# A new order of work at seven places of a split-fp32 hybrid decoder block

## The chip, the cores and the metric

The kernel runs on one core of one Trainium2 chip. The metric is the device time of one execution in microseconds (us). Before the change three runs gave 1134.07, 1134.16 and 1134.71; the median is 1134.16. The engines are named as in the profile: PE is TensorE (PEld its weight loads), DVE is VectorE, ACT is ScalarE, POOL is GpSimd, SP is SyncE, which issues most transfers.

## The reference, cut to what matters

```python
h = concatenate([meta, x], axis=1)              # 16 meta tokens + 512 tokens, 1024 wide
h = h + 0.5 * swiglu(rmsnorm(h, ffn1_norm), w1, w3, w2)
hn = rmsnorm(h, mix_norm)
q, k, v, u, g_attn, g_ssm = split(hn @ w_in, SPLITS)
attn = sliding_window_attention(q, k, v, attn_sinks)   # 16 query heads, 4 key heads, window 128
y = gelu(s5_ssm(u, ...))
ssm = (y @ ssm_glu_a) * sigmoid(y @ ssm_glu_b)
merged = sigmoid(g_attn) * attn + sigmoid(g_ssm) * ssm
h = h + merged @ w_out
h = h + 0.5 * swiglu(rmsnorm(h, ffn2_norm), w1, w3, w2)  # second set of weights
return rmsnorm(h, final_norm)[:, N_META:]
```

`swiglu(h, w1, w3, w2)` is `(silu(h @ w1) * (h @ w3)) @ w2`, and the hidden width is 2816 (22 tiles of 128).

## The kernel before, in words

All large matrices are multiplied in three parts. An fp32 operand is split into a high part (a copy rounded by ScalarE, tags `whi`, `hgh`, `gh`, `YH`, `KH`) and a low part (the difference, mostly by VectorE: `wlo`, `hgl`, `gl`, `YL`, `KL`). Each product is then high by high, low by high and high by low, three matmuls in one PSUM tile (`mm3`, lines 218 to 231). Activations lie transposed: 128 rows of the model width per tile, 528 columns (512 tokens and 16 meta tokens, as two halves of 264 with 8 meta columns each); behind the meta tokens' last use there are 512.

The weights stream through the core. `load_raw` (line 149) lets SP fetch one block into one of two raw buffers; `prep_piece` splits 128 of its columns, ScalarE the high part (line 166), then VectorE the low part (line 167), into one of three buffers; the last piece of a block also requests the next block. A unit is the work on one piece: `step` issues its matmuls, splits a later piece, and evacuates PSUM. Pieces of other work, the `mids`, are put between a unit's matmuls at even distances (`accumulate`). Each engine runs its own instructions in exactly the order in which the program issues them, so the place of a call in the program decides who stands behind whom. A PSUM tile that ScalarE and VectorE both read is read by one after the other, in program order; a tile that is taken again waits for its last reader.

The stages, with the lines that the change and the prediction touch:

- Head (about 0 to 44 us). `warm` (line 734) issues matmuls on a tile of ones, two instructions a call, in three places with counts `WARM`. The input `x` arrives in four row blocks `xb`; `x_t` (line 763) transposes two 128-column tiles of two row blocks into one of four PSUM buffers tagged "ax" (a pool that other small products share, in turn); `x_hi` (line 767, ScalarE) and `x_lo` (line 771, VectorE) make the split, gain-scaled activations from it, and `x_cp` (lines 778 and 780) copies the plain transposes to `hT`. `x_meta` (line 745) does this for the meta tokens, with one half of the tile that `warm` writes. `first_mm` (line 851) holds the first two units, w1 and w3 of the first hidden tile: unit 0 on column half 0, then unit 1 on half 0, unit 0 on half 1, and unit 1 on half 1, 96 matmuls counted c = 0 to 95. The dictionary of `first_work` names what is issued ahead of which count: the transposes and splits of half 1, the squares of the rows (`sq`, lines 869 and 871), the evacuation of unit 0 (`keep_p`, line 858, into `held0`), the split of the third piece, the copies `x_cp`, and the meta tokens' sums (`sums`, line 884), whose "ax" tile is the next in turn. In unit 2, `diag_r` (line 318) and `bcast_r` (lines 325 to 328) spread each row's norm factor over the partitions, and `small` (lines 862 to 865) brings in the other gains and the sinks.
- Rest of FFN1, then the projections of the mixer (k, v, u), and the state-space layer. `ssm_f` (lines 1094 to 1101) transposes its result and splits it into `YH` and `YL`.
- Mixer units (about 500 to 718 us): 30 units of 24 matmuls of 512 columns, for q, the gates and the two GLU products, in the order `MIX`. Each has 11 cuts, at which the parts of the attention are issued: scores (`s1`, lines 1249 to 1252), softmax (`s3`, with line 1267), transposes and values. `ksplit` (lines 1197 to 1201) splits one key tile, that is two key heads e = 0 and 1, four ScalarE copies and four low parts; `qsplit` (lines 1226 and 1227) does it for query tiles, high parts on ScalarE, low parts on GpSimd. `ksplit(0)` and two `qsplit` stand ahead of the units, `ksplit(1)` in unit 8. Every unit but the first splits one later piece at cut 8. The last units' `msplit` (lines 1389 and 1390) splits the merged result (`merge`, line 1335) for w_out; `glu`'s evacuation is lines 1380 and 1381.
- w_out, FFN2, and the tail (from about 1100 us). The last product is made by column halves in 16 steps j: `tail_mm` (line 1501), evacuation `tail_evac` (lines 1506 to 1517, which scales by the final gain into `zg`, one of five buffers), and transposes back `tail_t` (line 1525), each two steps behind its `tail_evac` in the first half. `tail_out` scales the rows and writes them.

Of the kernel before, what the change touches and what calls it, by code (L numbers as in the profile page):

```python
# [21 lines left out]
CHUNKS2 = [6, 6, 6, 4]  # L22
WARM = (6, 4, 3)
MIX = (
# [4 lines left out]
)  # L29
NCUT = 11  # L30
KS1 = 8
VS = (1, 0, 2, 10, 13, 13)
# [7 lines left out]
T = 8  # L40
# [12 lines left out]
def fr(ap):  # L53
    return ap.bitcast(F32)
# [3 lines left out]
def hybrid_block_kernel(  # L58
# [752 lines left out]
    m_lo = x_meta()  # L811
    warm(WARM[2])
    x_t(0, 2)
# [93 lines left out]
    def first_work():  # L907

        w = {}

        def at(c, f, *a):
            w.setdefault(c, []).append(lambda: f(*a))
        at(24, sums_meta)
        for g in range(2):
            for j in range(2 * g, 2 * g + 2):
                at(28 + 8 * g, x_t, 1, j)
            for d in range(4 * g, 4 * g + 4):
                at(28 + 8 * g, x_hi, 1, d)
                at(28 + 8 * g, x_lo, 1, d)
        for b in range(4):  # L920
            at(52, sq, b)
        at(72, keep_p, 0)
        at(74, prep_piece)
        for j in range(4):
            at(76, x_cp, 1, j, V if j % 2 else S)
        at(80, sums)
        return w

    pairs = first_downs(CHUNKS1)
    for i, u in enumerate(units):  # L930
        mids = ()
        if i == 0:
            work = first_work()
        elif i == 2:
            mids = (lambda: dgs.append(diag_r(x_p)), lambda: bcast_r(ax_ps, dgs[0]), small)
        elif i > 3:
            mids = (lambda: next(side, None),)
        if i in pairs:
            step2(u, units[i + 1], mids)
        elif i - 1 not in pairs:  # L940
            step(*u, hold=i < 3, mids=mids, prep=i > 0)
        if i == 2:
            flush()
            sx.close()
    for _ in side:
# [144 lines left out]
    def ssm_f(b0, q):  # L1090
# [3 lines left out]
        for t in range(4):  # L1094
            PE.transpose(ps[:, 128 * t:128 * t + 128], y[:, 4 * q + t].rearrange("k g c -> k (g c)"), ident)
        src = ps.rearrange("p (t e k) -> p e k t", t=4, e=2)
        for e in range(2):
            oh = YH[:, b0 + e, :].rearrange("p (k t) -> p k t", t=T)[:, :, 4 * q:4 * q + 4]
            ol = YL[:, b0 + e, :].rearrange("p (k t) -> p k t", t=T)[:, :, 4 * q:4 * q + 4]
            S.activation(out=oh, in_=src[:, e], func=AF.Copy)  # L1100
            V.tensor_tensor(out=ol, in0=src[:, e], in1=fr(oh), op=ALU.subtract)

# [88 lines left out]

    def ksplit(m):
        t = kT[m].rearrange("p h c -> p (h c)")
        for e in range(2):
            r = slice(64 * e, 64 * e + 64)
            o = slice(64 - 64 * e, 128 - 64 * e)
            S.activation(out=KH[r, 2 * m + e, :], in_=t[r], func=AF.Copy)
            S.activation(out=KH[o, 2 * m + e, :], in_=t[r], func=AF.Copy)
            eng = G if m else V
            eng.tensor_tensor(out=KL[r, 2 * m + e, :], in0=t[r], in1=fr(KH[r, 2 * m + e, :]), op=ALU.subtract)  # L1200
# [190 lines left out]

    ksplit(0)
    for m in range(2):
# [6 lines left out]
    for i, u in enumerate(units):  # L1400
# [19 lines left out]
        at_cut(CUT["ev"], flush)  # L1420
        at_cut(CUT["ev2"], flush2)
        if i == KS1:
            at_cut(CUT["ks"], ksplit, 1)
            at_cut(CUT["ks"], vmeta, 1)
        for v, iv in enumerate(VS):
            if i == iv:
                at_cut(CUT["vs"], vsplit, *divmod(v, 3))
        if i:
            at_cut(CUT["prep"], prep_piece)
# [4 lines left out]

        step(*u, mids=[lambda fs=fs: [f() for f in fs] for fs in cuts], prep=False, hold=i < len(units) - 1)


# [118 lines left out]
    for j in range(2 * ND):  # L1556
# [9 lines left out]
        tail_evac(p, h, d)  # L1566
        for t in after.get(j, (j - 2,) if 2 <= j < 8 else ()):
            if t not in (14, 15):
                tail_t(*divmod(t, ND))
# [36 lines left out]
```

## Time and profile before

| | |
|---|---|
| median of three runs | 1134.16 us |
| profiled execution | 1134.81 us |
| its span, first to last instruction | 1133.0 us |
| mean granted PE clock | 0.996 |
| PE, PEld, DVE, ACT, POOL busy | 99%, 89%, 56%, 36%, 32% of the span |
| bytes moved by DMA | 108.43 MB, 96 GB/s |

A row of a timeline or a group reads: start or none, busy time, engine, line, operation, output from inputs, partitions by elements and type, count, and in square brackets how long the engine stood idle ahead of it and what released it. Busy times of matmuls that overlap are longer than the step from one start to the next. "issue" as a releaser means that the profile shows nothing that the engine waited for.

### The profile page before, as it was taken

To read this page: it belongs to the slowest core of one execution; us is meant where nothing else is said; L and a number is where in the kernel's file an instruction comes from. 1 tells how busy PE (TensorE), PEld (TensorE's weight loads), DVE (VectorE), ACT (ScalarE), POOL (GpSimd) and SP (SyncE) were. 2 spreads that over 40 slices of the span, in tenths; PEclk is the share of its full clock that TensorE was granted. 3 is DMA by queue.
4 is the path that set the end of the run, shared out by engine and by line. 5 is a ranking of instruction groups with operands and counts; after the bars stand their busy time and mean duration, and the time that the engine had idled before them with its cause. 6 is when DMAs were issued, how large, how long until landed. Compare 5 with 4: busy or idle time off the path is not lost.

```text
span 1133.0 us, 17255 instructions
## 1 busy us (share of the span) xinstructions
PE 1117.9 (99%) x7012; PEld 1004.0 (89%) x7012; DVE 633.4 (56%) x963; ACT 409.2 (36%) x726; POOL 360.4 (32%) x488
## 2 busy tenths in 40 slices
PE   8999999999999999999999999999999999999997
PEld 7999999999999999978888888888888888888887
DVE  5546663655444363878777786554444444444454
ACT  5322232232222242456656555343322222222233
POOL 1777672542884031535455231130000000000003
PEclk9999999999999999999999999999999999999998
DMA  5523233232423246122222212423232223323222
GB/s 155 147 76 111 75 95 113 75 86 84 113 76 102 76 139 200 49 75 75 75 75 70 76 52 101 149 76 110 93 116 89 86 98 114 112 63 123 75 75 75
DMA packets 105903, 108.43 MB, mean 96 GB/s; under 512 B 7568, under 2 KB 102032, under 8 KB 105696
## 3 DMA queue, kind: packets, MB, share of 16 engines
q1 hardware_dynamic: 103424, 100.74, 28.4%
q0 software_dynamic: 2352, 6.52, 2.2%
q8 instruction: 55, 0.90, 0.3%
q14 instruction: 24, 0.20, 0.1%
q10 hardware_dynamic: 48, 0.07, 0.0%
HBM read 100.80 MB, written 5.34 MB: 94 GB/s over the span
## 4 chain that ended last, share of the span: by engine, by line
PE 91%; DVE 4%; ACT 2%; issue 1%; POOL 1%; POOLq 0%; DVEq 0%; ACTq 0%
PE p L231 63%; PE p L405 11%; PE p L407 9%; PE p L1501 1%; PE pv L1310 1%; PE ps_t L1275 1%; DVE wlo L167 1%; PE ps_s L1249 1%; PE ps_s L1250 1%; PE p L851 1%; PE ps L734 1%; DVE hgl L771 0%; POOL qs L1227 0%; ACT hgh L767 0%; ACT whi L166 0%
## 5 line engine op out<-in xcount | busy, mean ns | idle before, releaser
L231 PE MATMUL p<-hgh,whi 128*128 128x264 f32 (+1 forms) x1408 | 403.8, 333 | 0.1
L231 PE MATMUL p<-hgl,whi 128*128 128x264 f32 (+1 forms) x1408 | 402.8, 332 | 0.2 <-DVE hgl L1390 0.2
L231 PE MATMUL p<-hgh,wlo 128*128 128x264 f32 (+1 forms) x1408 | 401.0, 331 | 0.0
L167 DVE TENSOR_TENSOR wlo<-raw,whi 128x1024 fp32r<-128x1024 f32 (+2 forms) x190 | 250.1, 1316 | 84.3 <-ACT whi L166 81.9
L231 PEld LDWEIGHTS p<-hgh,whi 128*128 128x128 f32 x1408 | 239.0, 188 | 26.5 <-issue 1.1
L231 PEld LDWEIGHTS p<-hgh,wlo 128*128 128x128 f32 x1408 | 238.6, 189 | 23.3
L231 PEld LDWEIGHTS p<-hgl,whi 128*128 128x128 f32 x1408 | 238.8, 189 | 22.7 <-DVE hgl L1390 0.5
L166 ACT ACTIVATE whi<-raw 128x1024 fp32r<-128x1024 f32 (+2 forms) x190 | 185.5, 978 | 127.4 <-PE p L407 72.2
L1517 POOL TENSOR_TENSOR acc<-acc,zq 128x256 f32<-128x256 f32 x12 | 8.8, 735 | 349.8 <-ACT zq L1510 349.7
L377 ACT ACTIVATE t<-t 128x528 f32<-128x528 f32 (+1 forms) x44 | 28.1, 639 | 167.0 <-DVE t L376 167.0
L425 DVE SCALAR_TENSOR_TENSOR hT<-p,hT 128x528 f32<-128x528 f32 (+1 forms) x56 | 39.1, 698 | 87.5 <-PE p L407 52.2
L387 ACT ACTIVATE gh<-t 128x528 fp32r<-128x528 f32 (+1 forms) x44 | 28.1, 639 | 161.9 <-DVE t L386 161.9
L405 PE MATMUL p<-gh,whi 128*128 128x264 f32 x352 | 72.5, 287 | 0.7 <-DVE hT L425 0.5
L405 PE MATMUL p<-gl,whi 128*128 128x264 f32 x352 | 71.4, 284 | 0.0
L405 PE MATMUL p<-gh,wlo 128*128 128x264 f32 x352 | 71.4, 284 | 0.0
L376 DVE TENSOR_TENSOR t<-p,r_bc 128x512 f32<-128x512 f32 (+1 forms) x43 | 30.0, 698 | 69.3 <-PE p L231 69.1
L386 DVE TENSOR_TENSOR t<-p,t 128x512 f32<-128x512 f32 (+1 forms) x43 | 30.0, 698 | 66.7 <-PE p L231 66.3
L405 PEld LDWEIGHTS p<-gh,whi 128*128 128x128 f32 x352 | 54.5, 188 | 1.9 <-issue 0.8
L407 PE MATMUL p<-gh,whi 128*128 128x512 f32 x144 | 56.0, 389 | 0.0
L407 PE MATMUL p<-gl,whi 128*128 128x512 f32 x144 | 56.0, 389 | 0.0
L407 PE MATMUL p<-gh,wlo 128*128 128x512 f32 x144 | 56.0, 389 | 0.0
L378 DVE TENSOR_TENSOR t<-t,r_bc 128x528 f32<-128x528 f32 (+1 forms) x44 | 37.3, 848 | 32.4 <-ACT t L377 32.4
(331 smaller groups left out, 1500.3 us busy)
## 6 DMA issues: line engine op xcount, KB each, us to landing
raw<-in_ffn_w_dram SPq DMA_DIRECT2D x42, 1024.0 KB, 5.4
raw<-in_ffn_w_dram SPq DMA_DIRECT2D x24, 768.0 KB, 4.2
raw<-in_w_in_dram SPq DMA_DIRECT2D x16, 1024.0 KB, 5.6
raw<-in_ffn_w_dram SPq DMA_DIRECT2D x10, 512.0 KB, 3.6
raw<-in_w_out_dram SPq DMA_DIRECT2D x4, 1024.0 KB, 5.1
h_keep<-hT POOLq DMA_DIRECT2D x1, 2112.0 KB, 7.3
xb<-in_x_dram SPq DMA_DIRECT2D x8, 256.0 KB, 5.1
raw<-in_ssm_glu_a_dram SPq DMA_DIRECT2D x4, 512.0 KB, 3.5
```

The costliest lines, as they stand in the source:

```text
L166: S.activation(out=hi, in_=src, func=AF.Copy)
L167: V.tensor_tensor(out=lo, in0=src, in1=fr(hi), op=ALU.subtract)
L231: PE.matmul(out=o, lhsT=w[:, k0 + k, :], rhs=sl(r, k), start=start, stop=stop)
L376: V.tensor_tensor(out=t1, in0=cell[1], in1=rb(), op=ALU.mult)
L377: S.activation(out=t1, in_=t1, func=AF.Silu)
L378: V.tensor_tensor(out=t1, in0=t1, in1=rb(), op=ALU.mult)
L386: V.tensor_tensor(out=t3, in0=cell[3], in1=cell["t1"], op=ALU.mult)
L387: S.activation(out=gh, in_=t3, func=AF.Copy)
L405: PE.matmul(out=p[:, h, :HALF], lhsT=wt[:, k, :], rhs=gs[k][c][:, h, :], start=start, stop=stop)
L407: PE.matmul(out=p, lhsT=wt[:, k, :], rhs=gs[k][c].rearrange("p h c -> p (h c)"), start=start, stop=stop)
L425: V.scalar_tensor_tensor(out=hv(hT, d), in0=cell["p"], scalar=0.5, in1=hv(hT, d), op0=ALU.mult, op1=ALU.add)
L734: PE.matmul(out=ps_0[:, 0, 0:128], lhsT=ones, rhs=ones, start=True, stop=True)
```

## The change

1. `WARM` goes from (6, 4, 3) to (6, 2): two of the four calls ahead of the first transposes go, and the third group, ahead of `x_t(0, 2)`, goes altogether.
2. In `first_work`, the four high parts of each group of half 1 come ahead of their four low parts; they alternated. `x_cp` of half 1 moves from c = 76 to 50, the split of the third piece from 74 to 52, the squares from 52 to 54, `sums` from 80 to 88.
3. In unit 2 `diag_r` stays at its quarter, `bcast_r` moves from a half to three quarters, and `small` moves to the middle of unit 3. The head's pool is closed one unit later.
4. `ssm_f` makes both high parts ahead of both low parts.
5. `ksplit(0)` ahead of the mixer units does only key head e = 0. Head e = 1 follows at cut 10 of mixer unit 3 (counted from 0), its low parts on GpSimd instead of VectorE.
6. The last mixer unit no longer splits a piece at cut 8; that piece is split behind the unit's evacuation.
7. The tail's transposes run three steps behind `tail_evac` instead of two, up to j = 8.

```diff
@@ -20,7 +20,7 @@
 EPS = 1e-6
 CHUNKS1 = [4, 6, 6, 6]
 CHUNKS2 = [6, 6, 6, 4]
-WARM = (6, 4, 3)
+WARM = (6, 2)
 MIX = (
     ("q", 1), ("gs", 0), ("glu", 0), ("q", 2), ("ga", 0),
     ("gs", 1), ("glu", 1), ("q", 3), ("ga", 1),
@@ -28,6 +28,7 @@
     ("gs", 3), ("ga", 3), ("glu", 3),
 )
 NCUT = 11
+KS0 = 3
 KS1 = 8
 VS = (1, 0, 2, 10, 13, 13)
 CUT = {"s3": 5, "s3m": 7, "s3e": 7, "ev2": 6, "s1": (2, 4, 7, 7), "s2o": 7, "s2p": 7, "s2m": 8, "prep": 8, "ev": 0, "ks": 10, "vs": 7}
@@ -809,7 +810,6 @@
     x_lo(0, 0)
     x_lo(0, 1)
     m_lo = x_meta()
-    warm(WARM[2])
     x_t(0, 2)
     x_t(0, 3)
     x_lo(0, 2)
@@ -914,16 +914,16 @@
         for g in range(2):
             for j in range(2 * g, 2 * g + 2):
                 at(28 + 8 * g, x_t, 1, j)
-            for d in range(4 * g, 4 * g + 4):
-                at(28 + 8 * g, x_hi, 1, d)
-                at(28 + 8 * g, x_lo, 1, d)
+            for f in (x_hi, x_lo):
+                for d in range(4 * g, 4 * g + 4):
+                    at(28 + 8 * g, f, 1, d)
+        for j in range(4):
+            at(50, x_cp, 1, j, V if j % 2 else S)
+        at(52, prep_piece)
         for b in range(4):
-            at(52, sq, b)
+            at(54, sq, b)
         at(72, keep_p, 0)
-        at(74, prep_piece)
-        for j in range(4):
-            at(76, x_cp, 1, j, V if j % 2 else S)
-        at(80, sums)
+        at(88, sums)
         return w
 
     pairs = first_downs(CHUNKS1)
@@ -932,7 +932,9 @@
         if i == 0:
             work = first_work()
         elif i == 2:
-            mids = (lambda: dgs.append(diag_r(x_p)), lambda: bcast_r(ax_ps, dgs[0]), small)
+            mids = (lambda: dgs.append(diag_r(x_p)), lambda: None, lambda: bcast_r(ax_ps, dgs[0]))
+        elif i == 3:
+            mids = (small,)
         elif i > 3:
             mids = (lambda: next(side, None),)
         if i in pairs:
@@ -941,6 +943,7 @@
             step(*u, hold=i < 3, mids=mids, prep=i > 0)
         if i == 2:
             flush()
+        if i == 3:
             sx.close()
     for _ in side:
         pass
@@ -1094,11 +1097,11 @@
         for t in range(4):
             PE.transpose(ps[:, 128 * t:128 * t + 128], y[:, 4 * q + t].rearrange("k g c -> k (g c)"), ident)
         src = ps.rearrange("p (t e k) -> p e k t", t=4, e=2)
+        oh, ol = [[t[:, b0 + e, :].rearrange("p (k t) -> p k t", t=T)[:, :, 4 * q:4 * q + 4] for e in range(2)] for t in (YH, YL)]
         for e in range(2):
-            oh = YH[:, b0 + e, :].rearrange("p (k t) -> p k t", t=T)[:, :, 4 * q:4 * q + 4]
-            ol = YL[:, b0 + e, :].rearrange("p (k t) -> p k t", t=T)[:, :, 4 * q:4 * q + 4]
-            S.activation(out=oh, in_=src[:, e], func=AF.Copy)
-            V.tensor_tensor(out=ol, in0=src[:, e], in1=fr(oh), op=ALU.subtract)
+            S.activation(out=oh[e], in_=src[:, e], func=AF.Copy)
+        for e in range(2):
+            V.tensor_tensor(out=ol[e], in0=src[:, e], in1=fr(oh[e]), op=ALU.subtract)
 
     def st2():
         s = stats(sqs, ax_ps)
@@ -1189,14 +1192,14 @@
 
     V.tensor_reduce(out=hm, in_=ident.rearrange("p (l h k) -> p h l k", l=2, h=4), axis=mybir.AxisListType.XY, op=ALU.add)
 
-    def ksplit(m):
+    def ksplit(m, es=(0, 1)):
         t = kT[m].rearrange("p h c -> p (h c)")
-        for e in range(2):
+        for e in es:
             r = slice(64 * e, 64 * e + 64)
             o = slice(64 - 64 * e, 128 - 64 * e)
             S.activation(out=KH[r, 2 * m + e, :], in_=t[r], func=AF.Copy)
             S.activation(out=KH[o, 2 * m + e, :], in_=t[r], func=AF.Copy)
-            eng = G if m else V
+            eng = G if m or e else V
             eng.tensor_tensor(out=KL[r, 2 * m + e, :], in0=t[r], in1=fr(KH[r, 2 * m + e, :]), op=ALU.subtract)
             eng.tensor_tensor(out=KL[o, 2 * m + e, :], in0=t[r], in1=fr(KH[r, 2 * m + e, :]), op=ALU.subtract)
 
@@ -1389,7 +1392,7 @@
         S.activation(out=mg[0][:, m, :], in_=AT[:, m, :], func=AF.Copy)
         V.tensor_tensor(out=mg[1][:, m, :], in0=AT[:, m, :], in1=fr(mg[0][:, m, :]), op=ALU.subtract)
 
-    ksplit(0)
+    ksplit(0, (0,))
     for m in range(2):
         qsplit(m, qT[m])
     units = []
@@ -1419,13 +1422,15 @@
                 at_cut(CUT[c], f, begin[i - 1])
         at_cut(CUT["ev"], flush)
         at_cut(CUT["ev2"], flush2)
+        if i == KS0:
+            at_cut(CUT["ks"], ksplit, 0, (1,))
         if i == KS1:
             at_cut(CUT["ks"], ksplit, 1)
             at_cut(CUT["ks"], vmeta, 1)
         for v, iv in enumerate(VS):
             if i == iv:
                 at_cut(CUT["vs"], vsplit, *divmod(v, 3))
-        if i:
+        if 0 < i < len(units) - 1:
             at_cut(CUT["prep"], prep_piece)
         if i == len(units) - 2:
             mg += new_hg(SEQ)
@@ -1433,6 +1438,7 @@
                 at_cut(m, msplit, m)
 
         step(*u, mids=[lambda fs=fs: [f() for f in fs] for fs in cuts], prep=False, hold=i < len(units) - 1)
+    prep_piece()
 
 
     at.close()
@@ -1564,7 +1570,7 @@
         if j == 2 * ND - 1:
             tail_t(1, d - 1)
         tail_evac(p, h, d)
-        for t in after.get(j, (j - 2,) if 2 <= j < 8 else ()):
+        for t in after.get(j, (j - 3,) if 3 <= j < 9 else ()):
             if t not in (14, 15):
                 tail_t(*divmod(t, ND))
         if j == 9:
```

Lines of the changed kernel lie 1 to 6 higher. The three places below show what stands in an engine's row before and after; the numbers behind names are buffer numbers.

ScalarE in the head, from the last high parts of half 1 (`hgh`) to the weight split ahead of unit 2; `whi_353` and `whi_325` are the third piece, `ps_x_266` and `ps_x_261` the tile of `x_t(1, 0)`. Before:

```order
L767 ACTIVATE hgh_104<-ps_x_297,gT_66 128x256 [waits PE_49]
L767 ACTIVATE hgh_104<-ps_x_297,gT_66 128x256 [waits DVE_49]
L869 ACTIVATE xb1_112,ssq_88<-xb1_112 128x1024 [waits DMAHW5_49,DMAHW3_49,Pool_49]
L869 ACTIVATE xb3_114,ssq_88<-xb3_114 128x1024 [waits DMAHW5_49,DMAHW3_49]
L858 ACTIVATE held0_221<-p_231 128x528 [waits PE_49]
L166 ACTIVATE whi_353<-raw_211 128x1024 [waits DMAHW6_49]
L778 ACTIVATE hT_93<-ps_x_266 128x2x256
L778 ACTIVATE hT_93<-ps_x_292 128x2x256
L858 ACTIVATE held1_222<-p_256 128x528 [waits PE_49]
L166 ACTIVATE whi_392<-raw_215 128x1024 [waits DMAHW7_49,Activation_49]
```

After:

```order
L768 ACTIVATE hgh_104<-ps_x_292,gT_66 128x256 [waits PE_49]
L768 ACTIVATE hgh_104<-ps_x_292,gT_66 128x256
L779 ACTIVATE hT_93<-ps_x_261 128x2x256 [waits DVE_49]
L779 ACTIVATE hT_93<-ps_x_287 128x2x256 [waits DVE_49]
L167 ACTIVATE whi_325<-raw_206 128x1024 [waits DMAHW6_49]
L869 ACTIVATE xb1_112,ssq_88<-xb1_112 128x1024 [waits DMAHW5_49,DMAHW3_49,Pool_49]
L869 ACTIVATE xb3_114,ssq_88<-xb3_114 128x1024 [waits DMAHW5_49,DMAHW3_49]
L858 ACTIVATE held0_216<-p_226 128x528 [waits PE_49]
L858 ACTIVATE held1_217<-p_251 128x528 [waits PE_49]
L167 ACTIVATE whi_387<-raw_210 128x1024 [waits DMAHW7_49,Activation_49]
```

The two copies to `hT` stood behind the squares, `held0` and the third piece; they now stand directly behind the last high part, the third piece behind them, and the squares and `held0` last. The last high part waits for PE alone, no longer for VectorE.

ScalarE at the start of the mixer units, the last `ssm_f` parts (`YH`), the key tile (`KH`) and the first two query tiles (`qs`). Before:

```order
L1100 ACTIVATE YH_4773<-psT_5641 128x64x4 [waits PE_49]
L1100 ACTIVATE YH_4773<-psT_5641 128x64x4 [waits DVE_49]
L1100 ACTIVATE YH_4773<-psT_5650 128x64x4 [waits PE_49]
L1100 ACTIVATE YH_4773<-psT_5650 128x64x4 [waits DVE_49]
L1197 ACTIVATE KH_5679<-kT_5140 64x544 [waits DMAHW7_49,DMAHW2_49]
L1198 ACTIVATE KH_5679<-kT_5140 64x544
L1226 ACTIVATE qs_5712<-tq0_5564 64x512 x2
L1226 ACTIVATE qs_5717<-tq0_5635 64x512 x2
```

The two lines of `KH` stand there twice, once for each key head. After:

```order
L1102 ACTIVATE YH_4768<-psT_5636 128x64x4 [waits PE_49]
L1102 ACTIVATE YH_4768<-psT_5636 128x64x4
L1102 ACTIVATE YH_4768<-psT_5645 128x64x4 [waits PE_49]
L1102 ACTIVATE YH_4768<-psT_5645 128x64x4
L1200 ACTIVATE KH_5674<-kT_5135 64x544 [waits DMAHW7_49,DMAHW2_49]
L1201 ACTIVATE KH_5674<-kT_5135 64x544
L1229 ACTIVATE qs_5703<-tq0_5559 64x512 [waits DVE_49]
L1229 ACTIVATE qs_5703<-tq0_5559 64x512
L1229 ACTIVATE qs_5708<-tq0_5630 64x512 [waits DVE_49]
L1229 ACTIVATE qs_5708<-tq0_5630 64x512
```

The second high part of each pair no longer waits for VectorE, and two of the four copies to `KH` are gone from this place.

VectorE in the last mixer unit: GLU evacuation (`tg`, `ts`), merge (`AT`), the last low part for w_out (`hgl`) and weight splits (`wlo`). Before:

```order
L167 TENSOR_TENSOR wlo_7823<-raw_7660,whi_7822 128x1024 [waits Activation_49]
L1380 SCALAR_TENSOR_TENSOR tg_7813<-tg_7813,p_7815 128x512 [waits PE_49]
L1381 SCALAR_TENSOR_TENSOR ts_7671<-ts_7671,tg_7813 128x512 [waits DVE_49]
L1335 SCALAR_TENSOR_TENSOR AT_5683<-ts_7671,AT_5683 128x512 [waits DVE_49]
L1390 TENSOR_TENSOR hgl_7746<-AT_5683,hgh_7745 128x512 [waits Activation_49]
L167 TENSOR_TENSOR wlo_7898<-raw_7737,whi_7897 128x1024 [waits DMAHW1_49,Activation_49]
```

After:

```order
L1393 TENSOR_TENSOR hgl_7741<-AT_5678,hgh_7740 128x512 [waits Activation_49]
L1383 SCALAR_TENSOR_TENSOR tg_7808<-tg_7808,p_7810 128x512 [waits PE_49,Activation_49]
L1384 SCALAR_TENSOR_TENSOR ts_7666<-ts_7666,tg_7808 128x512 [waits DVE_49]
L1338 SCALAR_TENSOR_TENSOR AT_5678<-ts_7666,AT_5678 128x512 [waits DVE_49]
L1393 TENSOR_TENSOR hgl_7741<-AT_5678,hgh_7740 128x512 [waits Activation_49]
L168 TENSOR_TENSOR wlo_7829<-raw_7655,whi_7828 128x1024 [waits Activation_49]
L168 TENSOR_TENSOR wlo_7893<-raw_7732,whi_7892 128x1024 [waits DMAHW1_49,Activation_49]
```

The first `wlo` moved from ahead of the GLU evacuation to behind the low part `hgl`.

## The prediction

> **What bounds the kernel now.** I read the page first, and on it the chain that ended last, by engine.
>
> ```profile
> PE 91%; DVE 4%; ACT 2%; issue 1%; POOL 1%; POOLq 0%; DVEq 0%; ACTq 0%
> ```
>
> PE carries 91% of the chain, and the change removes only four plain matmuls from it and three more at a place where PE waits. So a gain can only come from stretches in which PE waits, or runs at a lower clock. I therefore went through PE's starts in the timeline for steps longer than its usual .23 us for 512 columns or .12 for 264, and asked at each place what released it. The places that the change touches are the head (0 to 35 us), the first attention scores (504 to 508), the end of the mixer (718) and the tail (1106). Of the clock, the stretches of 3.41 us say most; their columns are length, busy time of PE, PEld, DVE, ACT and POOL, granted clock, DMA share and GB/s.
>
> ```profile
> 0.00:3.59 3.59, 2.59 (x12) 2.59 (x12) 0.00 (x0) 1.49 (x2) 2.70 (x13) 1.00 0.47 143
> 3.59:7.00 3.41, 3.15 (x15) 2.83 (x15) 0.17 (x1) 0.00 (x0) 0.52 (x2) 1.00 0.91 261
> 7.00:10.41 3.41, 2.40 (x24) 2.14 (x23) 2.24 (x7) 2.40 (x6) 0.96 (x3) 1.00 1.15 318
> 10.41:13.82 3.41, 2.87 (x23) 2.45 (x20) 3.05 (x8) 3.15 (x8) 0.77 (x2) 1.00 0.59 217
> 24.07:27.48 3.41, 1.68 (x16) 1.57 (x16) 2.66 (x5) 2.23 (x4) 0.00 (x0) 1.00 0.00 0
> 27.48:30.89 3.41, 3.41 (x18) 3.41 (x17) 0.95 (x4) 1.55 (x2) 2.69 (x4) 0.50 0.90 286
> ```
>
> The clock is 0.50 in exactly one stretch of 3.41 us, right behind the one stretch in which PE was busy for only 1.68 of 3.41. A stretch with 2.40 busy (7.00 to 10.41) was followed by full clock.
>
> **The change part by part.** All sums are made against the profiled execution, 1134.81 us (1.8 of it lie around the span), which is .65 above the median 1134.16 and .1 above the slowest of the three timed runs.
>
> Term 1, the warm-up calls in the head:
>
> ```profile
> 4.39 2.07 PE L734 MATMUL ps<-ones 128*128 128x128 f32 x8 [0.26 <-DVE gT L738]
> 6.25 1.41 PE L763 MATMUL ps_x<-ident,xb 128*128 128x128 f32 x8
> 9.26 0.94 PE L734 MATMUL ps<-ones 128*128 128x128 f32 x6 [1.01 <-DVE hT L750]
> 10.67 1.57 ACT L767 ACTIVATE hgh<-ps_x,gT 128x256 fp32r<-128x256 f32 x4 [0.27 <-PE ps_x L763]
> 1.17 0.42 SPq L717 DMA_DIRECT2D xb<-in_x_dram  x1
> xb<-in_x_dram SPq DMA_DIRECT2D x1, 256.0 KB, 4.2
> ```
>
> A call counts as two instructions. Eight of them fill 4.39 to 6.25, so four are .93; the first transposes can start about .9 earlier, at 5.4, where the second x transfer (issued at 1.17, landing 4.2 later) arrives as well. ScalarE's first high parts, and all that hangs on them, move with them. The third call made PE wait 1.01 for VectorE's copy out of the same tile; without it the next transposes are ready early, and ScalarE's wait of .27 goes. Together at most 1.1; I take 1.0. The low bound is .2 (rival 1).
>
> Term 2, high parts ahead of low parts, and term 3, the copies `x_cp` ahead of the squares:
>
> ```profile
> 21.10 0.52 PE L851 MATMUL p<-hgh,whi 128*128 128x264 f32 x3
> 21.86 0.39 PE L851 MATMUL p<-hgh,whi 128*128 128x264 f32 x1 [0.24 <-ACT hgh L767]
> 23.05 1.13 PE L851 MATMUL p<-hgh,whi 128*128 128x264 f32 x8
> 25.23 0.59 ACT L778 ACTIVATE hT<-ps_x 128x512 f32<-128x512 f32 x1
> 25.92 0.24 PE L884 MATMUL ps_mq<-ones,mq 128*8 128x1 f32 x4 [1.73 <-issue]
> ```
>
> PE's fourth matmul would have followed at 21.10 + 3 x .12 = 21.46; it came at 21.86, since each ScalarE high part waited for the VectorE low part of the same PSUM tile. With four high parts in a row that .4 goes (bounds 0, if another part is late, and .5).
>
> The wait of 1.73 before line 884 is put down to "issue", so I looked for who frees its tile. `sums` takes the fourth "ax" buffer in turn, that of ps_x(1,0), whose last reader is the ScalarE copy of line 778: it ends at 25.23 + .59 = 25.82, and PE goes on at 25.92. The copy stood behind two squares, `held0` and a weight's high part. It now stands ahead of them. PE's eight matmuls from 23.05 at .1225 end their issue at 24.03, so 25.92 - 24.03 = 1.9 goes (bounds 1.7, the wait as labelled, and 2.0). What is late next is `held0`, now behind both squares; unit 2 needs its PSUM buffer only after the rest of unit 1, by my count of these durations about 1 us later. `sums` itself moves from 80 to 88, and the squares it needs are done by then.
>
> Term 4, the half clock that follows:
>
> ```profile
> 29.96 0.64 PE L231 MATMUL p<-hgh,whi 128*128 128x264 f32 x2
> 30.41 0.63 PE L231 MATMUL p<-hgl,whi 128*128 128x264 f32 x2
> 31.36 0.40 PE L231 MATMUL p<-hgl,whi 128*128 128x264 f32 x2
> 31.60 0.41 PE L231 MATMUL p<-hgh,wlo 128*128 128x264 f32 x2
> ```
>
> Two matmuls take 30.41 - 29.96 = .45 at half clock and 31.60 - 31.36 = .24 at full clock. The stretch of 3.41 us costs 3.41 x (1 - .24/.45) = 1.6. With the gap of 1.9 gone, the stretch before it is about 3.4 busy instead of 1.68, so I expect the clock to stay, worth 1.5 (bounds 0 and 1.6). The Trainium skill, page "TensorE: Matmul & The Clock Gate", section "HAM oscillation — how this bites in real kernels", has it that only idle gaps longer than about 3.4 us lower the clock; by that rule a gap of 1.9 would not have done it, its removal would not save the 1.5, and the sum would come to 5.85 instead of 7.35. The trace sides with the gap, as the two rows of 1.68 and 0.50 stand next to each other; rival 2 keeps the other case.
>
> The broadcast moves from the middle of unit 2 to its third quarter:
>
> ```profile
> 32.58 0.59 PE L325 MATMUL ps_r<-dg,ones 128*128 128x256 f32 x2
> 34.36 0.51 PE L231 MATMUL p<-hgh,whi 128*128 128x264 f32 x2
> ```
>
> It occupies PE for 34.36 - 32.58 = 1.8 wherever it stands; `small` too only moves. Since unit 2 starts some 4 us earlier while the row factors do not, the broadcast may wait for VectorE's diagonal, 0 to .5; I take 0, as the quarter of a unit of 24 x .24 us gives it 1.4 more. The head gives 1.0 + .4 + 1.9 + 1.5 = 4.8.
>
> Term 5, the attention's start:
>
> ```profile
> 497.60 0.66 ACT L1100 ACTIVATE YH<-psT 128x256 fp32r<-128x256 f32 x2 [1.36 <-DVE YL L1101]
> 499.08 0.65 ACT L1197 ACTIVATE KH<-kT 64x544 fp32r<-64x544 f32 x1
> 502.54 8.07 POOL L1227 TENSOR_TENSOR qs<-tq,qs 64x512 fp32r<-64x512 f32 x6 [12.81 <-ACT qs L1226]
> 503.89 0.33 PE L1249 MATMUL ps_s<-KH,qs 128*128 128x144 f32 x1 [0.58 <-POOL qs L1227]
> 507.95 0.33 PE L1249 MATMUL ps_s<-KH,qs 128*128 128x144 f32 x1 [0.65 <-POOL qs L1227]
> PEld ps_s L1249 <- POOL qs L1227: 2.2, 3, 1.0
> L1200 POOL TENSOR_TENSOR KL<-kT,KH x2: 1360/1536/1711, 567.2 to 570.4; 64x544 fp32r<-64x544 f32 x2
> 529.32 0.63 ACT L1362 ACTIVATE ts<-ts 128x512 f32<-128x512 f32 x1 [2.13 <-DVE ts L1361]
> 534.09 1.90 POOL L1267 TENSOR_TENSOR E<-E,den 128x1024 f32<-128x1024 f32 x1 [4.51 <-ACT ph L1278]
> ```
>
> PE waits .58 and .65 for GpSimd, whose low parts begin at 502.54 after ScalarE. Two of four key copies (.65 each) and waits for VectorE such as the 1.36 leave ScalarE's way to `qs`: it gets there about 3 us earlier, more than PE's waits. So .58 + .65 and a restart of about .1 at each go: 1.4 (bounds 1.2 and the weight loads' 2.2). The second head's parts return in the fourth unit: 2 x .65 on ScalarE, 2 x 1.54 = 3.1 on GpSimd. Queued behind them are the softmax steps; the idle 2.13 and 4.51 in front of 529.32 and 534.09 hide them.
>
> Term 6, the last mixer weight, and term 7, the tail:
>
> ```profile
> 713.57 1.23 DVE L167 TENSOR_TENSOR wlo<-raw,whi 128x1024 fp32r<-128x1024 f32 x1 [0.74 <-ACT whi L166]
> 717.54 0.69 DVE L1390 TENSOR_TENSOR hgl<-AT,hgh 128x512 fp32r<-128x512 f32 x1 [0.70 <-ACT hgh L1389]
> 717.56 0.50 PE L231 MATMUL p<-hgh,whi 128*128 128x512 f32 x1
> 718.29 0.50 PE L231 MATMUL p<-hgl,whi 128*128 128x512 f32 x1 [0.22 <-DVE hgl L1390]
> 1105.34 0.41 DVE L1506 SCALAR_TENSOR_TENSOR z<-p,hT 128x256 f32<-128x256 f32 x1
> 1105.57 0.28 PE L1501 MATMUL p<-gh,hgl 128*128 128x256 f32 x1
> 1106.19 0.44 PE L1525 MATMUL ps_z<-ident,zg 128*128 128x128 f32 x2 [0.35 <-DVE zg L1515]
> ```
>
> The merge and the last low part no longer stand behind a 1.23 us weight part on VectorE. PE's second matmul came .73 after the first instead of .23: .5, with the restart .6 (bounds .5 and .7). The moved weight part ends about when the merge chain ended, before PE's second w_out unit; its raw tile's successor is requested some 3 us later on SP, which has none waiting behind it.
>
> In the tail the transposes at 1106.19 waited for zg, .62 after the matmul of 1105.57 instead of .12. With a lag of three that zg is long there. Next late is the PSUM buffer that VectorE frees at 1105.34 + .41 = 1105.75, almost in time: .55 (bounds .3 and .65).
>
> Sum: 4.8 + 1.4 + .6 + .55 = 7.35. Profiled: 1127.5. Median: 1134.16 - 7.35 = 1126.8.
>
> **The rivals.** Rival 1: the clock rises later in the head, or falls again there. With four calls gone and PE idle until ScalarE delivers, the stretch 7.00 to 10.41 may hold about 2.1 us of work (2.40 less the .94 of the third call, and an estimated .6 of unit 0's matmuls, which start about 1.0 earlier), between the 2.40 that kept the clock and the 1.68 that lost it. Until 13.82, 18 matmuls of .225 instead of .12 cost 1.9; the rows to 13.82 show PE idle for 1.55 of it, so between .35 and 1.9, .8 taken: 1127.6. For it: 2.59 busy in the first stretch did not raise it (at 4.39 an instruction still took .23). Against: 2.1 is nearer 2.40. The Trainium skill, the same page, section "Part 4: PE-mode transpose", says that transposes do not count as PE-busy; by that the eight transposes from 6.25 on would not help, and this rival would be the forecast; here the stretch of 7.00 to 10.41, full of transposes, kept the clock.
>
> Rival 2: the gap did not cause the half clock, and 1.5 stays: 1128.3. Rival 3: the change does not do what it says there, since the wait labelled "issue" is not the copy's: terms 3 and 4 stay, 1130.2; against it stand 25.82 and 25.92. Rival 4: the second key head's 3.1 us on GpSimd delay the softmax by all of it: 1129.9; against it the idle 4.51.
>
> Rival 5, slower: the clock, once not raised in the head, stays at half through several stretches, because PE, waiting for ScalarE and VectorE, never fills one. A matmul then costs (.45 - .24)/2 = .105 more; to lose the 7.35 and 2.3 besides takes 92 of them, at half clock from 9.8 to 30.4, six stretches. If it lasts to 34.3, 109 matmuls cost 11.4: 1138.2. Against it: the rows to 30.89 show only one such stretch, behind 1.68.
>
> **How the numbers follow.** Forecast .56, rival 1 .22, rival 2 .08, rival 3 .06, rival 4 .05, rival 5 .03. All terms at their high ends give 8.75, 1125.4; that is the low end. The high end is rival 3's 1130.2, near the low ends' sum (.2 + 1.7 + 1.2 + .5 + .3 = 3.9, 1130.3). About 2.3 us, .2%, is what a measurement of this kernel can tell from no change: faster than 1131.9 has .94 (all but rival 5, and .03 of rivals 3 and 4 with a new wait, which are "same"), slower .03.
>
> **What would show it.** Right: no PE gap at `sums`, clock 1.00 from 14 to 31, unit 2 starting about 4 us earlier, no wait for qs at the first scores, none for hgl at the first w_out unit, 1106's wait gone. Wrong: a half clock between 10 and 31, a PE wait for `held0`'s tile or for dg, GpSimd waits in mixer units 4 to 7.

## The result and the profile after

Four runs of the changed kernel took 1126.15, 1126.45, 1126.64 and 1126.71 us, median 1126.55; four of the kernel before 1134.07 to 1134.71, median 1134.29. The ratio is 0.9931, with a 95% interval of 0.9915 to 0.9947: 7.7 us faster. Executions of 1220 us and more, the profiled one of e5 among them (granted clock .65), are left out of every comparison below. The page of the profiled execution (1126.45 us) answers with a shorter span, and PE's share of the chain that ended last went from 91 to 96%; the waits for DVE, ACT, POOL and "issue" are what became less.

```profile
span 1124.7 us, 17248 instructions
PE 96%; DVE 2%; ACT 1%; issue 0%; DMA 0%; POOLq 0%; POOL 0%; DVEq 0%; SPq 0%; ACTq 0%
```

The stretches of 3.41 us of the changed kernel: in the second row and the third PE is busy throughout and the clock is granted in full, where the kernel before had 1.68 busy and then 0.50. The first row belongs to the head; there the trace's clock records set the clock to full at 4.15 us, in the kernel before at 7.00. Ahead of its first record the column reads 1.00 all the same: in the kernel before, instructions of the warm-up still took .23 us each at 4.39, inside a row that reads 1.00.

```profile
0.74:4.15 3.41, 3.13 (x13) 2.81 (x13) 0.00 (x0) 1.49 (x2) 3.03 (x10) 1.00 0.59 170
24.07:27.48 3.41, 3.41 (x30) 3.41 (x29) 1.22 (x2) 1.56 (x2) 3.36 (x5) 1.00 0.60 205
27.48:30.89 3.41, 3.41 (x23) 2.70 (x22) 1.06 (x7) 0.52 (x2) 0.04 (x1) 1.00 0.66 185
```

The timeline of PE in the head:

```profile
4.39 0.71 PE L735 MATMUL ps<-ones 128*128 128x128 f32 x4 [0.26 <-DVE gT L739]
9.47 0.75 PE L851 MATMUL p<-hgh,whi 128*128 128x264 f32 x4 [0.92 <-ACT whi L797]
23.22 0.25 PE L884 MATMUL ps_mq<-ones,mq 128*8 128x1 f32 x4
24.47 0.40 PE L232 MATMUL p<-hgh,whi 128*128 128x264 f32 x2
28.87 0.59 PE L326 MATMUL ps_r<-dg,ones 128*128 128x256 f32 x2
```

The first split matmul starts at 9.47 (10.82 before) and waits for ScalarE's weight part; `sums` (line 884) and the broadcast (line 326) follow with no wait; unit 2 starts at 24.47. The timelines of GpSimd and PE at the first scores, of PE at the first w_out unit, and of DVE and PE in the tail:

```profile
493.53 8.62 POOL L1230 TENSOR_TENSOR qs<-tq,qs 64x512 fp32r<-64x512 f32 x6 [9.26 <-ACT qs L1229]
497.67 0.23 PE L1252 MATMUL ps_s<-KH,qs 128*128 128x144 f32 x1
500.61 0.28 PE L1252 MATMUL ps_s<-KH,qs 128*128 128x144 f32 x1
710.31 0.39 PE L232 MATMUL p<-hgl,whi 128*128 128x512 f32 x1
1097.26 0.41 DVE L1512 SCALAR_TENSOR_TENSOR z<-p,hT 128x256 f32<-128x256 f32 x1
1097.81 0.35 PE L1507 MATMUL p<-gh,hgh 128*128 128x256 f32 x1 [0.24 <-DVE z L1512]
```

The query tiles' low parts begin 4.1 us ahead of the first score instead of 1.35, the waits at the scores and at 710.31 are gone, and in the tail one wait has taken another's place: PE now waits for VectorE's `z`, which frees a PSUM buffer.

To see where the time went, I took each PE instruction that both kernels have, in program order, and subtracted its start after from its start before:

| up to this PE instruction | before | after | earlier by | new since the row above |
|---|---|---|---|---|
| first split matmul of unit 0 | 10.82 | 9.47 | 1.36 | 1.36, term 1 and the clock's earlier rise |
| first behind the old wait for `hgh` | 21.86 | 20.09 | 1.77 | .4, term 2 |
| behind `sums` | 27.28 | 23.63 | 3.66 | 1.9, term 3 |
| FFN1, past all that moved | 68.04 | 63.01 | 5.03 | 1.4, term 4 and the broadcast |
| last ahead of the first score | 502.93 | 497.43 | 5.49 | .5, in no term |
| behind the first scores | 508.71 | 501.31 | 7.40 | 1.9, term 5 |
| behind the first w_out matmuls | 719.10 | 710.99 | 8.10 | .6, term 6 (.08 drift ahead of it) |
| late tail | 1112.04 | 1103.67 | 8.37 | .3, term 7 |

The .5 in no term arises between 405 and 471 us, most of it where the state-space layer waits for VectorE. e7, e9 and e10 below have the changed kernel's order there, and lost .3 to .4 of it again in their traces, so I count it as scatter of one execution.

### The profile page after: what moved, and what is told of

Read it like the earlier page. It is cut to its first block, busy times and chain, and to the rows that moved or that the text cites. A ratio compares the mean times of both kernels' runs of the same rounds, so it can differ in the third digit from the quotient of the medians.

```text
span 1124.7 us, 17248 instructions
## 1 busy us (share of the span) xinstructions
PE 1113.1 (99%) x7002; PEld 1000.2 (89%) x7002; DVE 633.4 (56%) x961; ACT 409.1 (36%) x726; POOL 361.8 (32%) x490
## 4 chain that ended last, share of the span: by engine, by line
PE 96%; DVE 2%; ACT 1%; issue 0%; DMA 0%; POOLq 0%; POOL 0%; DVEq 0%; SPq 0%; ACTq 0%
PE p L232 67%; PE p L406 11%; PE p L408 9%; PE p L1507 1%; PE pv L1313 1%; PE ps_t L1278 1%; PE p L851 1%; PE ps_s L1252 1%; PE ps_s L1253 1%; PE psS L1029 1%; DMA xb<-in_x_dram 0%; PE psY L1087 0%; PE psY L1085 0%; PE pv L1321 0%; PE psW L667 0%
```

## The experiments

All times are medians. The kernel before lay at 1134.18 to 1134.33 in the comparisons below. The first six take the head apart. Two executions can differ in the head without an edit: e2 and e4, whose edits lie further back, start unit 0 1.1 and 1.2 us earlier than the trace of before, since the clock rose at 4.63 and 3.86 instead of 7.00. What an edit did is therefore read from where the difference of PE's starts changes, not from the whole of it.

**e1: the copy alone.** `x_cp(1, 0)` goes to c = 50 in the kernel before:

```diff
+        at(50, x_cp, 1, 0, S)
-        for j in range(4):
+        for j in range(1, 4):
             at(76, x_cp, 1, j, V if j % 2 else S)
```

> The kernel before, with one ScalarE copy (x_cp(1, 0)) issued ahead of the squares instead of behind the third piece's split; nothing else moves. My theory (this copy frees the tile of sums, and the gap it causes costs the clock the next 3.41 us): the wait of 1.73 us at sums goes, the clock stays 1.00 from 24 to 31 us, 1.9 + 1.5 = 3.4 us less, about 1130.9. Rival 2 (the gap did not cause the half clock): only 1.9 less, about 1132.4, with a stretch of 3.41 us at 0.50 still there. Rival 3 (the wait is not the copy's): the wait stays at 1.7 and the time at about 1134.3.

Measured: 1135.47, ratio 1.0012 (1.0003 to 1.0022), slower by about 1 us. The wait at `sums` did go, and `sums` started 1.95 us earlier, so rival 3 is out; but PE's timeline shows a new wait, and the stretches behind it two at half clock:

```profile
31.45 0.67 PE L325 MATMUL ps_r<-dg,ones 128*128 128x256 f32 x2 [1.78 <-DVE dg L318]
```

```profile
27.06:30.47 3.41, 2.61 (x20) 2.40 (x20) 2.41 (x5) 0.89 (x1) 1.95 (x1) 1.00 0.64 198
30.47:33.89 3.42, 2.44 (x12) 1.76 (x13) 1.13 (x6) 0.87 (x3) 2.31 (x5) 1.00 1.10 356
33.89:37.30 3.41, 3.41 (x17) 3.11 (x16) 0.74 (x3) 0.86 (x1) 0.62 (x1) 0.50 0.25 70
37.30:40.72 3.42, 3.42 (x17) 3.42 (x17) 2.67 (x4) 0.65 (x1) 3.42 (x5) 0.50 0.42 131
```

The broadcast at the half of unit 2 now came before the diagonal of the row factors: 1.78 of the 1.95 were paid back there, and the half clock came behind that gap. None of the three forecasts had this. The ten runs fall into two groups, five of 1133.85 to 1134.66 with a mean clock of .996 to .998 and five of 1136.29 to 1137.24 with .993 to .995; the trace (1136.60) is of the second, so the two half stretches are not in every run.

**e11: the copy and the broadcast's place.** As e1, and `bcast_r` at three quarters of unit 2, `small` in unit 3, as in the change:

```diff
-            mids = (..., lambda: bcast_r(ax_ps, dgs[0]), small)
+            mids = (..., lambda: None, lambda: bcast_r(ax_ps, dgs[0]))
+        elif i == 3:
+            mids = (small,)
```

> The kernel before with the early copy x_cp(1, 0) and, besides, the broadcast at three quarters of unit 2 and small in unit 3. The early copy alone took the wait at sums away (1.95 us) and paid it back at the broadcast (1.78 us for the diagonal, and two stretches at half clock). Theory (the copy and the broadcast's move are one step together): the broadcast waits .5 us or less, the clock stays at 1.00 behind 14 us in most executions, 2.0 to 3.4 us less than before, 1130.9 to 1132.4. Rival (the row factors are late whatever the place, as DVE's work ahead of the diagonal has only been moved): the wait of 1.8 us moves with it, about 1134.3.

Measured: 1131.86, ratio 0.9983 (0.9973 to 0.9992): 2.3 us less than before, where e1 was 1.1 more. Of the 1.78 the waits list keeps .3, and the clock holds (no half stretch in the trace, a mean clock of .998 in all ten runs):

```profile
PE ps_r L325 <- DVE dg L318: 0.3, 1, 0.3
```

So the copy takes the gap away, and the broadcast's move keeps it away. It is 2.3 and not the 3.4 of terms 3 and 4: the .3 shows that the diagonal is still a little late here even at three quarters, and where the rest went stays open.

**e9: the broadcast's place in the changed kernel.** Only the two entries of `mids` are swapped, so that the broadcast stands at the half again.

```diff
-            mids = (..., lambda: None, lambda: bcast_r(ax_ps, dgs[0]))
+            mids = (..., lambda: bcast_r(ax_ps, dgs[0]), lambda: None)
```

> The changed kernel with the broadcast at the half of unit 2 instead of three quarters. The forecast priced the move at nothing. The kernel before with the early copy alone showed a wait of 1.78 us for the diagonal there. Theory (the move is what keeps terms 3 and 4): the broadcast is due at 27.4 us, the diagonal is ready at 28.5, so PE waits about 1.1 us, 1127.7, and in executions where that falls into one stretch with more idle time the clock falls too, up to 1129.3. Rival (the diagonal is early enough): 1126.6.

Measured: 1128.02 (three runs of 1127.18 to 1128.36). In the trace the broadcast waits for the diagonal again, by less than I expected (.37; PE's later starts fall back by .64); another .7 was lost in the head, .5 of it from 9.8 to 13.3 us:

```profile
28.65 0.70 PE L326 MATMUL ps_r<-dg,ones 128*128 128x256 f32 x2 [0.37 <-DVE dg L319]
```

```profile
6.48:9.90 3.42, 2.32 (x21) 1.89 (x21) 2.48 (x8) 2.66 (x7) 1.18 (x3) 1.00 1.16 318
9.90:13.31 3.41, 3.41 (x17) 3.41 (x17) 3.41 (x8) 3.41 (x9) 0.55 (x1) 0.50 0.69 251
```

These two rows are rival 1, in one execution: a stretch with 2.32 busy and the clock halved behind it, for .5 us (priced at .8). Nothing in the edit lies there; the head is that of the changed kernel. Behind the broadcast's wait the clock stayed in full. So in the changed kernel the move is worth about .6, far less than the step from e1 to e11: VectorE begins the diagonal at 28.12 here and at 30.76 in e1; the rest of the head's new order, it seems, brings it forward too. The rows of VectorE, first here, then in e1:

```profile
28.12 1.13 DVE L319 TENSOR_SCALAR dg<-ident,rcol 128x128 f32<-128x128 f32 x6
30.76 1.13 DVE L318 TENSOR_SCALAR dg<-ident,rcol 128x128 f32<-128x128 f32 x6 [1.26 <-POOL rcol L312]
```

**e2: the gap filled, not removed.** In the kernel before, eight `PE.matmul` of ones into unused PSUM columns ahead of `sums`. They compute nothing that is read.

```diff
+        at(80, fill)
         at(80, sums)
```

> The kernel before, with eight extra matmuls of ones (sixteen instructions of .11 us, 1.8 us) put ahead of sums, into PSUM columns that nothing reads: the wait for the copy stays as long, but PE is busy in it. My theory (low busy time in one stretch lowers the clock in the next): clock 1.00 from 24 to 31, 1.5 us less, about 1132.8. Rival 2 (the half clock has another cause): the half clock stays, 1134.3 or up to .2 more.

Measured: 1132.89, 1.4 less than before by the medians (ratio 0.9991, 0.9981 to 1.0). The wait for the copy is still there, only filled; the clock stays:

```profile
21.70:25.10 3.40, 3.40 (x33) 3.25 (x32) 2.65 (x5) 3.40 (x7) 0.00 (x0) 1.00 0.00 0
25.10:28.50 3.40, 3.40 (x29) 3.40 (x30) 1.81 (x5) 1.37 (x3) 1.41 (x2) 1.00 0.50 133
```

That is term 4 by itself, and rival 2 is out: the idle time lowers the clock. None of the ten runs lies above 1133.74, while 39 of 48 runs of the kernel before lie at 1133.9 or more (see e3). A part of the gain is lost again: the broadcast, due earlier, waits for the diagonal here, and by the same .47 in the traces of e3 and e4.

```profile
30.58 0.67 PE L325 MATMUL ps_r<-dg,ones 128*128 128x256 f32 x2 [0.47 <-DVE dg L318]
```

**e3: the warm-up alone.** `WARM = (6, 2)` and no third group, in the kernel before.

```diff
-WARM = (6, 4, 3)
+WARM = (6, 2)
-    warm(WARM[2])
```

> The kernel before with WARM (6, 2) and without the third warm-up group; nothing else. My theory: the first split matmul of unit 0 (10.82 us before) comes 1.0 to 1.4 us earlier, and so does everything behind it, about 1133.2; the wait at sums and the half clock behind it stay. Rival 1 (the clock rises later for want of warm-up): the head start shrinks to .2, with matmuls at .22 us after 9 us, about 1134.1.

Measured: 1133.24, 1.1 less by the medians, but with an interval that includes no change (ratio 0.9994, 0.9984 to 1.0003). In the trace unit 0 starts 1.13 earlier, with the clock's rise at 7.00 us as in the trace of before. Here the wait at `sums` stood, and yet no half clock followed in this execution:

```profile
PE ps_mq L883 <- issue: 1.7, 1, 1.7
```

```profile
20.65:24.07 3.42, 2.36 (x17) 2.15 (x17) 2.77 (x5) 3.42 (x7) 0.00 (x0) 1.00 0.00 0
24.07:27.48 3.41, 2.68 (x24) 2.68 (x25) 2.65 (x5) 1.38 (x4) 0.40 (x1) 1.00 0.22 37
```

The gap, 1.1 us earlier, fell across the border of two stretches, and neither was empty enough. A gap of one length may or may not cost the clock, by where it falls. The kernel before seems to show the same in its own runs: of 48 in the comparisons here, 39 took 1133.9 to 1134.9 with a mean clock of .996 to .997, and 9 took 1132.5 to 1133.0 with .998. The 1.6 between them agrees with the price of one such stretch, and so does the clock, of which one half stretch takes 3.41 x .5 / 1133 = .0015; but these runs have no traces, and the traced execution (1134.81) is of the 39's kind.

**e4: high parts ahead of low parts alone.**

```diff
-                at(28 + 8 * g, x_hi, 1, d)
-                at(28 + 8 * g, x_lo, 1, d)
+            for f in (x_hi, x_lo):
+                for d in range(4 * g, 4 * g + 4):
+                    at(28 + 8 * g, f, 1, d)
```

> The kernel before with only the high parts of half 1 ahead of their low parts. My theory: the PE wait of .24 at 21.86 us goes, ScalarE runs four high parts back to back, everything behind comes .4 us earlier (up to .8 where the ScalarE chain sets the wait at sums): about 1133.8. Rival: the low parts are late instead, PE waits for VectorE, no gain: 1134.3.

Measured: 1131.94, ratio 0.998 (0.997 to 0.999), 2.4 less, where I had expected .5. In the trace the wait for `hgh` went (.46, as expected), and since ScalarE reached its copy earlier the wait at `sums` shrank too (by .6), so that no half clock followed:

```profile
PE ps_mq L884 <- issue: 1.2, 1, 1.2
```

```profile
20.92:24.33 3.41, 2.20 (x21) 1.99 (x20) 1.80 (x4) 2.53 (x4) 0.00 (x0) 1.00 0.00 0
```

The clock's stretch was worth 1.4 there, and .5 was lost again at the broadcast: .46 + .6 + 1.4 - .5 is 2.0 in the trace, for the 2.4 of the medians. The edits of the head are thus not worth a sum of their own prices: each of e2 and e4, and in some executions e3, brings the clock's 1.4 to 1.6 back, and it can be won only once.

**e5, e6: the two parts of term 5, each undone in the changed kernel.** The first puts `ssm_f` back to alternating parts, the second both key heads ahead of the mixer units. e5_again is the kernel of e5, run again for its trace.

```diff
 e5:                                              e6:
             S.activation(out=oh[e], ...)         -    ksplit(0, (0,))
-        for e in range(2):                       +    ksplit(0)
             V.tensor_tensor(out=ol[e], ...)      -        if i == KS0:
                                                  -            at_cut(CUT["ks"], ksplit, 0, (1,))
                                                  -            eng = G if m or e else V
                                                  +            eng = G if m else V
```

> The changed kernel with the high and low parts of ssm_f alternating again. Term 5 measured 2.0 us of PE starts at the three first scores. Theory A (the two parts of term 5 overlap: two key copies less on ScalarE are enough, as PE's three waits are .74, .22 and .92 us): no wait for GpSimd comes back or under .3, 1126.6. Theory B (both parts are needed): a wait of .5 to 1.5 us comes back, up to 1128.

> The kernel with the alternating ssm_f again, for its trace and more times: three times lay .9 us above the changed kernel's. Theory A (overlap, as with the key heads, whose undoing brought .33 us of PE starts back): under .4 us of PE starts at the first scores. Theory B (the order in ssm_f carries more of term 5 than the key head): .5 to 1.5 us there.

> The changed kernel with both key heads split ahead of the mixer units again, low parts on VectorE, none in the fourth unit. Theory A (overlap: the reordered ssm_f alone gets ScalarE to the query tiles nearly 2 us earlier): no wait or under .3, 1126.6. Theory B (both needed): .7 to 1.5 us of PE waits for GpSimd at the first scores come back, up to 1128. Rival 4 (the moved head costs something in the fourth unit): the time falls below 1126.

Measured: e5 1127.40 and 1127.33 (three runs each), e6 1126.91. Against the changed kernel's, PE's starts fall back across the first scores by .57 in e5_again (from .14 later to .71 later) and by .43 in e6 (from .04 earlier to .39 later), each by one wait for GpSimd. The waits of PE and the timeline of ScalarE, first of e5_again:

```profile
PE ps_s L1251 <- POOL qs L1229: 0.3, 1, 0.3
```

```profile
495.08 2.60 ACT L1228 ACTIVATE qs<-tq 64x512 fp32r<-64x512 f32 x4
```

Then of e6:

```profile
PE ps_s L1252 <- POOL qs L1230: 0.2, 1, 0.2
```

```profile
494.06 2.60 ACT L1229 ACTIVATE qs<-tq 64x512 fp32r<-64x512 f32 x4
```

ScalarE reaches the query tiles at 495.1 and 494.1, against 492.75 in the changed kernel. Together the two parts brought 1.9, undone one by one they cost .57 and .43: they overlap, as theory A had it, but not wholly; e5's .57 lies in theory B's range. That `ssm_f` is the larger rests on the medians (.8 above the changed kernel against .4) more than on these two traces. Rival 4 is out as well: e6, without the moved head, is not faster; the moved low parts lie in GpSimd's idle time, which in the changed kernel still has 1.78 us left ahead of the softmax step behind them (4.51 before):

```profile
526.65 1.90 POOL L1270 TENSOR_TENSOR E<-E,den 128x1024 f32<-128x1024 f32 x1 [1.78 <-ACT ph L1281]
```

**e7: terms 6 and 7 undone together**, in the changed kernel.

```diff
-        if 0 < i < len(units) - 1:
+        if 0 < i:
-    prep_piece()
-        for t in after.get(j, (j - 3,) if 3 <= j < 9 else ()):
+        for t in after.get(j, (j - 2,) if 2 <= j < 8 else ()):
```

> The changed kernel with terms 6 and 7 undone at once, which lie 380 us apart: the last mixer weight split ahead of the merge again, and the tail's transposes two steps behind. By the terms as forecast: .6 us back at the first w_out unit and .55 back in the tail, 1127.7. As the changed kernel's trace reads (a new wait of .5 us for VectorE's z at the same step of the tail): .64 back and .15 to .4 back, 1127.4.

Measured: 1127.86, 1.3 above the changed kernel's median, of which the trace shows .9: PE's starts fall back by .61 at the first w_out unit and by .29 in the tail. The old waits are back in its list of waits:

```profile
PE p L232 <- DVE hgl L1393: 0.2, 1, 0.2
PE ps_z L1530 <- DVE zg L1520: 0.3, 1, 0.3
```

**e12: transposes as warm-up**, in the changed kernel, to see whether they count for the clock.

```diff
-        for _ in range(n):
-            PE.matmul(out=ps_0[:, 0, 0:128], lhsT=ones, rhs=ones, start=True, stop=True)
+        for _ in range(2 * n):
+            PE.transpose(ps_0[:, 0, 0:128], ones, ident)
```

> The changed kernel with transposes of the tile of ones in place of the warm-up matmuls, as many instructions (twelve and four). If transposes count as work for the clock, it rises as in the changed kernel, at 4 to 7 us, and the time stays at 1126.6. If they do not count (the rule that the forecast cited beside rival 1), no stretch before 10 us is full enough, the clock rises only at 13 us or later, PE's matmuls up to there take .22 us, and the time rises by .7 to 2 us, 1127.3 to 1128.6.

Measured: 1128.16, 1.6 slower, but for a reason that I had overlooked: the transposes need `ident`, which GpSimd writes after `ones`, so PE starts at 2.65 instead of 1.00, and 1.5 is lost by the first split matmul.

```profile
2.65 2.82 PE L735 MATMUL ps<-ident,ones 128*128 128x128 f32 x12 [2.65 <-POOL ident L695]
```

```profile
0.67:4.08 3.41, 1.43 (x7) 1.43 (x8) 0.00 (x0) 1.49 (x2) 2.99 (x10) 1.00 0.63 179
4.08:7.49 3.41, 3.15 (x15) 2.73 (x14) 0.17 (x1) 0.00 (x0) 0.03 (x1) 1.00 0.91 254
```

The question is answered all the same: the clock rose at 7.49, at the end of a stretch in which PE did nothing but transposes.

**e10: two more moves.** The changed kernel with the first weight's high part ahead of the meta tokens' on ScalarE, and in the tail each weight's high part issued ahead of the evacuation, its low part behind it:

```diff
+    lows = [prep_half(0)]
     m_lo = x_meta()
...
-    lows = [prep_half(0)]
...
-        prep_piece()
+        low = prep_high()
...
         tail_evac(p, h, d)
+        low()
```

> The changed kernel with two more moves: in the head the first weight's first high part ahead of the meta tokens' on ScalarE (PE waits .9 us for it at 9.5 us), and in the tail each weight's high part issued ahead of the evacuation and its low part behind it (z stood behind a low part that waits for ScalarE, .4 us of PE). If both waits go without another taking their place: .5 and .4 us, 1125.7. If the meta tokens' parts, or the low part of the weight, are as late as the high part was: only the tail's .4, 1126.2. If the tail's low parts come too late for their matmuls: 1126.6 or more.

Measured: 1126.11 (1126.07 to 1126.30), .4 under the changed kernel's median; the ratio to before, 0.9932 (0.9916 to 0.9949), can't tell the two apart. In the trace the tail's wait for `z` is gone (.46 by PE's starts), and the head's gain of .54 at unit 0's first matmul is down to .08 by 13 us, as PE then waits for the meta tokens' high part and for the weight's low part:

```profile
8.92 0.75 PE L851 MATMUL p<-hgh,whi 128*128 128x264 f32 x4 [0.65 <-ACT hgh L753]
10.23 0.76 PE L851 MATMUL p<-hgh,wlo 128*128 128x264 f32 x4 [0.55 <-DVE wlo L800]
```

## Why the prediction was right, point by point

The forecast case came in, 1126.55 for 1126.8. In the two profiled executions the difference is 8.37, against a sum of 7.35; the medians differ by 7.7, as the profiled execution of before lay .5 above its median. That the sum came within .4 of the 7.7 is in part luck: term 5 brought .5 more than its price and term 7 .25 less, and what term 1 brings changes from execution to execution.

- **Term 1** (1.0): 1.36 in the difference, of which the edit's share hangs on when the clock rises. With the rise at 7.00 in both kernels it is 1.13 (e3 against before, 9.69 for 10.82). With a rise at 3.86 to 4.67 the old warm-up reaches its first split matmul at 9.64 to 9.71 (e2, e4, e11), the new one, with a rise at 4.15 to 4.59, at 9.01 to 9.47 (e6, e7, the changed kernel): .2 to .7 in these traces. The price of 1.0 was that of a late rise.
- **Term 2** (.4): .4.
- **Term 3** (1.9): 1.9. e1 shows that the "issue" wait was the copy's.
- **Term 4** (1.5): 1.4 in the difference; e2 shows the cause apart from the wait, and the two groups of times of the kernel before agree with its price. The size of the gap alone does not decide it, as e3 shows.
- **The broadcast** (0): right in its number, wrong in its reason. I priced the move as one that might add a wait. With the early copy alone it is what keeps terms 3 and 4: without it (e1) both are paid back at the diagonal, with it (e11) 2.3 stays. In the changed kernel it is worth about .6 (e9). The margin I gave it (a quarter of a unit, 1.4) was enough there, as the broadcast at 28.87 waits for nothing; in e11 it was .3 short.
- **Term 5** (1.4, bounds 1.2 and 2.2): 1.9. I had taken the idle time in front of two matmuls, .58 and .65. But there the weight load waits as well, and its overlap is lost besides: at three scores PE fell back by .84, .20 and .87 against the changed kernel, 1.9, and the second of them has no idle time of its own in PE's rows. The row of PEld's waits, 2.2 in three times, which I had kept as an upper bound, was the nearer one.
- **Term 6** (.6): .6, and .6 again in e7.
- **Term 7** (.55, bounds .3 and .65): .3, and .3 again in e7. The wait for `z` came where I had put it, but I compared two instructions with a different number of transposes ahead of them: with the longer lag one pair less has been done by then, and its .2 is paid later.
- **The rivals.** Rival 1 happened in one execution of e9, at .5 for the .8 given. Rival 2 fell by e2, rival 3 by e1, rival 4 by e6. Rival 5 was not seen: at most two half stretches in a row (e1).

## What to carry to other kernels

A wait that is taken away must be followed to the next place that depends on the same data: here the early copy alone only moved the wait to the broadcast, and copy and later broadcast together were worth 2.3 us. Where a weight load waits for the same data as its matmul, read the wait from the load's row, or from the step between matmul starts, not from the matmul's idle time. Gains that come over the clock are not to be added up: several edits can each bring the same lost stretch back, and an edit priced at .4 may move 2.4. And a difference between two traces holds the clock's phase as well as the edit: compare executions in which the clock rose at the same time, or many runs.

## What the runs showed of the hardware

The clock is set at the borders of stretches of 3.41 us (it changed at 7.00, 27.48 and 30.89 in before, at 6.48, 9.90 and 13.31 in e9), whose phase differs from execution to execution: its rise in the head came between 3.86 and 7.49 us in the traces here. In the head it rose behind stretches with 2.86 to 3.15 us of recorded PE time, and not behind 2.59 (before). Later a full stretch did not always do: in e1 a half stretch with 3.41 busy was followed by a second, while in before and e9 one was enough.

It fell behind stretches with 1.68 (before), 2.32 (e9) and 2.44 (e1), and did not fall behind 2.20 (e4), 2.33 (e12), 2.36 (e3) and 2.61 (e1). So the recorded busy time alone does not draw the line, nor does the kind of work: the 2.32 of e9 were transposes up to PE's wait of 1.10 us and one matmul behind it, e12's 2.33 transposes alone with 1.1 us idle behind them, and there the clock stayed in full. What does draw the line stays open. The rows of e12:

```profile
7.49:10.90 3.41, 2.33 (x22) 1.90 (x21) 2.19 (x7) 2.35 (x7) 0.90 (x3) 1.00 1.14 327
10.90:14.31 3.41, 2.99 (x18) 2.41 (x19) 3.41 (x8) 3.41 (x9) 0.83 (x2) 1.00 0.51 187
```

The Trainium skill, page "TensorE: Matmul & The Clock Gate", section "HAM oscillation — how this bites in real kernels", gives idle gaps of more than about 3.4 us as the condition; here the fall came behind stretches in which PE was idle for 1.73 (before), 1.10 (e9) and .98 us (e1, the second half of its wait), and the trace decides.

The Trainium skill, the same page, section "Part 4: PE-mode transpose", says that transposes don't count as PE-busy in the same way, and that the full clock doesn't engage for them; e12's clock rose behind a stretch of transposes alone, with 3.15 of 3.41 us recorded, which speaks against it here.
